# RMS normalisation on one core: last tile's load moved, squares, reductions and scaling dealt out anew

## The chip, the core and the metric

The kernel runs on one core of a Trainium2 chip. A core has TensorE (PE, matrix products), VectorE (DVE), ScalarE (ACT), GpSimd (POOL), SyncE (SP, which here only issues transfers) and 16 DMA engines, which move data between the main memory (HBM) and the on-chip memory SBUF. PSUM is a second, small on-chip memory; GpSimd is not used with it here. The engines run side by side and wait for each other by semaphores. The metric is the time of one execution on the device in microseconds (us), as the median of several runs.

## The reference

```python
batch, seq, dim = 16, 1024, 512      # x: float32; gamma: dim float32 values

def reference(x, gamma):
    eps = 1e-5
    rms = np.sqrt(np.mean(x ** 2, axis=-1, keepdims=True) + eps)
    return (x / rms * gamma).astype(np.float32)
```

Each of the 16384 rows of 512 values is divided by the root of its mean square and multiplied by gamma. 33.55 MB are read and 33.55 MB written.

## The kernel before

The 16384 rows are four tiles of 128 partitions x 32 rows x 512 values (64 KB per partition, 8 MB per tile). A partition's 32 rows lie one after the other in memory, so a transfer of n rows is 128 pieces of n x 2 KB. Three buffers `slot0` to `slot2` hold tiles 0, 1, 2; tile 3 uses `slot0` again, so its load must wait until tile 0 is stored.

All large transfers are issued by SP, in one queue: `load` (L42) and `store` (L45). SP works through its list in order, and a transfer whose data are not ready holds up what stands behind it. Their order is given by `transfers`: load 0 (8 rows, then 24), store row 0, load 1 (32), load 2 (16), store row 1 of tile 0, load 2 (16), store tile 0 (rows 2 to 32), store 1 (first 16), load 3 (16 and 16), store 1 (last 16), store 2 (32), store 3 (16 and 16).

A tile is worked on in four groups of 8 rows. For each group `row_stats` finds the sums of squares in one of two ways. In the first and third group of a tile ScalarE squares each row and accumulates its sum itself (L76, one instruction per row with an accumulator read behind it). In the second and fourth it squares four rows at a time into one of two PSUM buffers `sq` (L70), and VectorE adds them up (L71). ScalarE then takes the root (L82), and VectorE the reciprocal (L83). `apply` (L88) lets VectorE multiply each of the eight rows by its `rstd` and by `gamma_b`, in place, one instruction per row. gamma comes as one row by a small transfer; a matrix product with a column of ones spreads it over the partitions in PSUM, and VectorE copies it to `gamma_b` in SBUF (L57).

The main loop asks for the statistics of the next group ahead of scaling the current one. The order of instructions on each engine is that of a scheduler, which moves them within what the dependences allow: on VectorE, reductions and scaled rows of neighbouring groups are interleaved.

Of the kernel before, what the change touches and what calls it, by code (L numbers as in the profile page):

```python
# [1 line left out]

# [4 lines left out]


@with_exitstack
def kernel(  # L10
    ctx: ExitStack,
    tc: tile.TileContext,
    x: bass.AP,
    gamma: bass.AP,
    out: bass.AP,
):
    nc = tc.nc
    P = nc.NUM_PARTITIONS
    eps = 1e-5
    fp32 = mybir.dt.float32  # L20
    AF = mybir.ActivationFunctionType
    OP = mybir.AluOpType

    xf = x.flatten_outer_dims()
    of = out.flatten_outer_dims()
    N, D = xf.shape
    R = 32
    G = 8
    H = 4
    assert N == 4 * P * R  # L30

    xv = xf.rearrange("(t p r) d -> t p r d", p=P, r=R)
    ov = of.rearrange("(t p r) d -> t p r d", p=P, r=R)

    const = ctx.enter_context(tc.tile_pool(name="const", bufs=1))
    stats = ctx.enter_context(tc.tile_pool(name="stats", bufs=4))
    psum = ctx.enter_context(tc.tile_pool(name="psum", bufs=2, space=bass.MemoryType.PSUM))

    slots = [const.tile([P, R, D], fp32, name=f"slot{i}") for i in range(3)]

    def load(t, slot, r0, r1):
        nc.sync.dma_start(out=slots[slot][:, r0:r1], in_=xv[t][:, r0:r1])  # L42

    def store(t, slot, r0, r1):
        nc.sync.dma_start(out=ov[t][:, r0:r1], in_=slots[slot][:, r0:r1])  # L45

    load(0, 0, 0, 8)
    load(0, 0, 8, 32)

    gamma_row = const.tile([1, D], fp32)  # L50
    nc.scalar.dma_start(out=gamma_row, in_=gamma.unsqueeze(0))
    ones_col = const.tile([1, P], fp32)
    nc.vector.memset(ones_col, 1.0)  # L53
    gamma_psum = psum.tile([P, H, D], fp32, name="sq")
    nc.tensor.matmul(gamma_psum[:, 0], ones_col, gamma_row, start=True, stop=True)  # L55
    gamma_b = const.tile([P, D], fp32)
    nc.vector.tensor_copy(out=gamma_b, in_=gamma_psum[:, 0])  # L57

    eps_t = const.tile([P, 1], fp32)
    nc.vector.memset(eps_t, eps)  # L60
    sq_scratch = const.tile([P, D], fp32)

    def row_stats(slot, g):
        ss = stats.tile([P, G], fp32, name="ss")
        rms = stats.tile([P, G], fp32, name="rms")
        rstd = stats.tile([P, G], fp32, name="rstd")
        if (g // G) % 2:
            for h in range(0, G, H):
                sq = psum.tile([P, H, D], fp32, name="sq")
                nc.scalar.activation(out=sq, in_=slots[slot][:, g + h : g + h + H, :], func=AF.Square)  # L70
                nc.vector.tensor_reduce(  # L71
                    out=ss[:, h : h + H], in_=sq, axis=mybir.AxisListType.X, op=OP.add
                )
        else:
            for r in range(G):
                nc.scalar.activation(  # L76
                    out=sq_scratch,
                    in_=slots[slot][:, g + r, :],
                    func=AF.Square,
                    accum_out=ss[:, r : r + 1],  # L80
                )
        nc.scalar.activation(out=rms, in_=ss, func=AF.Sqrt, bias=eps_t, scale=1.0 / D)  # L82
        nc.vector.reciprocal(out=rstd, in_=rms)  # L83
        return rstd

    def apply(slot, g, rstd):
        for r in range(G):
            nc.vector.scalar_tensor_tensor(  # L88
                out=slots[slot][:, g + r, :],
                in0=slots[slot][:, g + r, :],  # L90
                scalar=rstd[:, r : r + 1],
                in1=gamma_b,
                op0=OP.mult,
                op1=OP.mult,
            )

    groups = [(t, g) for t in range(4) for g in range(0, R, G)]
    slot_of = [0, 1, 2, 0]

    def transfers(t, g):  # L100
        if (t, g) == (0, 0):
            store(0, 0, 0, 1)
            load(1, 1, 0, 32)
            load(2, 2, 0, 16)
            store(0, 0, 1, 2)
            load(2, 2, 16, 32)
        elif (t, g) == (0, 24):
            store(0, 0, 2, 32)
        elif (t, g) == (1, 8):
            store(1, 1, 0, 16)  # L110
            load(3, 0, 0, 16)
            load(3, 0, 16, 32)
        elif (t, g) == (1, 24):
            store(1, 1, 16, 32)
        elif (t, g) == (2, 24):
            store(2, 2, 0, 32)
        elif (t, g) == (3, 8):
            store(3, 0, 0, 16)
        elif (t, g) == (3, 24):
            store(3, 0, 16, 32)  # L120

    ahead = row_stats(0, 0)
    for k, (t, g) in enumerate(groups):
        rstd = ahead
        if k + 1 < len(groups):
            tn, gn = groups[k + 1]
            ahead = row_stats(slot_of[tn], gn)
        apply(slot_of[t], g, rstd)
        transfers(t, g)


# [1 line left out]
_INS = ['x', 'gamma']  # L133
_OUTS = [((16, 1024, 512), 'float32')]


# [23 lines left out]
```

## Time and profile before

| | us |
|---|---|
| median of 10 runs | 162.14 (161.91 to 162.45) |
| the profiled execution | 162.29 |
| its span (first to last record of the trace) | 160.5 |

| engine | busy in the span, us |
|---|---|
| VectorE: 128 scaled rows (L88) | 86.0 |
| VectorE: 16 reductions of 4 rows (L71) | 36.0 |
| ScalarE: 64 squares of one row (L76) and their 64 accumulator reads | 40.0 and 11.9 |
| ScalarE: 16 squares of 4 rows (L70) | 29.8 |
| ScalarE: 16 roots (L82) | 4.6 |

The busy time of a group is the sum of its instructions' own durations, which overlap a little: the next one starts before the last has quite ended. The DMA strip divides the span into 40 slices of 4 us and gives the mean busy share of the 16 DMA engines in tenths, 9 being 90% or more. The chain of waits follows the work that ended last back in time, at each step to what released it. It ends with the last compute instruction; a transfer issued after it is not in the chain.

Idle time that ScalarE spent waiting for VectorE's reductions (26.0 us before roots, 11.5 us before squares) and VectorE for ScalarE's roots (16.3 us) stands beside transfers that go on meanwhile.

### The profile page before, as it was taken

Reading aid. Unit: us, or ns where it says so; the run is one execution under the profiler, and the core shown is the slowest. Engines: PE = TensorE matmul, PEld = TensorE weight load, DVE = VectorE, ACT = ScalarE, POOL = GpSimd, SP = SyncE. Lnnn points to the kernel's source line nnn. Section 1 sums busy time; section 2 is a strip of 40 time slices with the busy share of each in tenths; the row PEclk is TensorE's granted clock in tenths of the full one; section 3 lists DMA queues with packets and bytes.
Section 4 is the critical chain, followed back from the end, with each engine's and each line's share of the span. In section 5 each row is a group of like instructions: output and inputs, shape, how many; then the busy total and the mean of one; then the engine's idle time right before and its main releaser. Section 6 shows DMA issues by size and latency. Waiting matters only on the chain.

```text
span 160.5 us, 409 instructions
## 1 busy us (share of the span) xinstructions
PE 2.0 (1%) x2; PEld 0.5 (0%) x2; DVE 122.6 (76%) x163; ACT 80.1 (50%) x162; POOL 0.2 (0%) x4
## 2 busy tenths in 40 slices
PE   3100000000000000000000000000000000000000
PEld 1000000000000000000000000000000000000000
DVE  0100937999999509999999999999999999995000
ACT  3099029991291999996900960079709940000000
POOL 0000000000000000000000000000000000000000
DMA  6999999699699999999899999999999899899993
GB/s 201 519 392 392 453 461 506 278 523 506 278 394 411 454 490 392 492 475 398 352 425 474 400 408 498 400 408 482 408 523 441 359 506 408 376 400 441 465 400 139
DMA packets 2164, 67.13 MB, mean 418 GB/s; under 512 B 241, under 2 KB 241, under 8 KB 498
## 3 DMA queue, kind: packets, MB, share of 16 engines
q1 hardware_dynamic: 2160, 67.11, 97.7%
q14 instruction: 2, 0.02, 0.0%
q10 hardware_dynamic: 2, 0.00, 0.0%
HBM read 33.56 MB, written 33.55 MB: 418 GB/s over the span
## 4 chain that ended last, share of the span: by engine, by line
DVE 64%; DMA 14%; ACT 11%; issue 2%; DVEq 0%; SPq 0%
DVE slot L88 45%; DVE ss L71 18%; DMA slot<-in_x_dram 14%; ACT sq_scratch L76 5%; ACT sq L70 5%; DVE rstd L83 1%; ACT rms L82 1%; DVEq L155 0%; SPq L42 0%
## 5 line engine op out<-in xcount | busy, mean ns | idle before, releaser
L88 DVE SCALAR_TENSOR_TENSOR slot<-slot,rstd,gamma_b 128x512 f32<-128x512 f32 x128 | 86.0, 748 | 0.1
L76 ACT ACTIVATE sq_scratch<-slot 128x512 f32<-128x512 f32 x64 | 40.0, 625 | 10.2 <-DMA slot<-in_x_dram 8.9
L70 ACT ACTIVATE sq<-slot 128x2048 f32<-128x2048 f32 x16 | 29.8, 1865 | 18.7 <-DVE ss L71 11.5
L71 DVE TENSOR_REDUCE ss<-sq 128x4 f32<-128x2048 f32 x16 | 36.0, 2284 | 3.5 <-ACT sq L70 3.5
L82 ACT ACTIVATE rms<-ss,eps_t 128x8 f32<-128x8 f32 x16 | 4.6, 297 | 26.2 <-DVE ss L71 26.0
L83 DVE RECIPROCAL rstd<-rms 128x8 f32<-128x8 f32 x16 | 3.2, 202 | 16.3 <-ACT rms L82 16.3
L76 ACT ACTIVATION_READ_ACCUMULATOR sq_scratch<-slot 128x1 f32 x64 | 11.9, 187 | 0.0
L57 DVE COPY gamma_b<-sq 128x512 f32<-128x512 f32 x1 | 0.7, 692 | 3.5 <-PE sq L55 3.5
L55 PE MATMUL sq<-gamma_row,ones_col 1*128 1x512 f32 x2 | 2.0, 1122 | 2.4 <-DMA gamma_row<-in_gamma_dram 2.4
L76 ACT ACT_TABLE_LOAD x1 | 1.3, 1283 | 1.3 <-PEq L144 1.3
L82 ACT ACT_TABLE_LOAD x1 | 1.3, 1283 | 0.0
L53 DVE MEMSET ones_col<- 1x128 f32 x1 | 0.2, 165 | 0.8 <-PEq L144 0.8
L55 PEld LDWEIGHTS sq<-gamma_row,ones_col 1*128 1x128 f32 x2 | 0.5, 306 | 2.4 <-issue 2.4
L144 POOL MEMSET const-bfloat16-1.0<- 128x1 bf16 x1 | 0.1, 101 | 0.0
L144 POOL MEMSET const-uint8-127<- 128x1 uint8 x1 | 0.1, 101 | 0.0
L144 POOL MEMSET const-float32-0.0<- 128x1 f32 x1 | 0.1, 98 | 0.2 <-issue 0.2
L144 POOL MEMSET const-float32-1.0<- 128x1 f32 x1 | 0.1, 98 | 0.0
L60 DVE MEMSET eps_t<- 128x1 f32 x1 | 0.1, 59 | 0.0
## 6 DMA issues: line engine op xcount, KB each, us to landing
slot<-in_x_dram SPq DMA_DIRECT2D x4, 4096.0 KB, 32.1
out_dram<-slot SPq DMA_DIRECT2D x4, 4096.0 KB, 18.5
out_dram<-slot SPq DMA_DIRECT2D x1, 7680.0 KB
slot<-in_x_dram SPq DMA_DIRECT2D x1, 6144.0 KB, 21.8
slot<-in_x_dram SPq DMA_DIRECT2D x1, 2048.0 KB, 7.4
out_dram<-slot SPq DMA_DIRECT2D x2, 256.0 KB, 21.2
gamma_row<-in_gamma_dram ACTq DMA_DIRECT2D x1, 2.0 KB
slot<-in_x_dram SPq DMA_DIRECT2D x1, 25.8
```

What stands on the lines that cost most here:

```text
L53: nc.vector.memset(ones_col, 1.0)
L55: nc.tensor.matmul(gamma_psum[:, 0], ones_col, gamma_row, start=True, stop=True)
L57: nc.vector.tensor_copy(out=gamma_b, in_=gamma_psum[:, 0])
L60: nc.vector.memset(eps_t, eps)
L70: nc.scalar.activation(out=sq, in_=slots[slot][:, g + h : g + h + H, :], func=AF.Square)
L71: nc.vector.tensor_reduce(out=ss[:, h : h + H], in_=sq, axis=mybir.AxisListType.X, op=OP.add)
L76: nc.scalar.activation(out=sq_scratch, in_=slots[slot][:, g + r, :], func=AF.Square, accum_out=ss[:, r : r + 1],)
L82: nc.scalar.activation(out=rms, in_=ss, func=AF.Sqrt, bias=eps_t, scale=1.0 / D)
L83: nc.vector.reciprocal(out=rstd, in_=rms)
L88: nc.vector.scalar_tensor_tensor(out=slots[slot][:, g + r, :], in0=slots[slot][:, g + r, :], scalar=rstd[:, r : r + 1], in1=gamma_b, op0=O ...
L144: nc = _bacc.Bacc("TRN2", target_bir_lowering=False, num_devices=1)
```

## The change

The order of instructions is now that of the source (`manual_schedule`), and VectorE's code begins at a multiple of 128 instruction slots (`addr_align`).

Work is dealt out anew. The groups are 8, 12 and 12 rows in tile 0 and 16 rows in the other tiles. ScalarE only squares, in pieces of 7, 5 and 4 rows, by turns into one PSUM buffer and one SBUF buffer, and takes the roots; the sums of all rows are VectorE's. Of each group the last rows (`share`: 3, 5, 5, 7, 7, 6, 6, 6, 3, in all 48 of 128) are scaled by GpSimd in two multiplications, by `rstd` and by gamma from SBUF. VectorE scales the others, one row per instruction as before, with gamma read from PSUM. ScalarE makes the SBUF copy of gamma, and GpSimd the two constants.

The transfers: the store of row 1 of tile 0 between the two halves of load 2 goes. Tile 0 is stored in rows 1 to 16 and 16 to 32, right after that tile 3 is loaded, then tile 1 is stored in one transfer of 128 pieces of 64 KB; tile 2 is stored in two halves.

```diff
+    ctx.enter_context(tc.manual_schedule())
+    nc.vector.addr_align(128, offset=0, max_nops=0)
...
-    nc.vector.tensor_copy(out=gamma_b, in_=gamma_psum[:, 0])
+    nc.scalar.copy(out=gamma_b[:, 0], in_=gamma_psum)
...
+    groups = [
+        (0, 0, 8, (4, 4), 3),
+        (0, 8, 12, (7, 5), 5),
+        (0, 20, 12, (7, 5), 5),
+        (1, 0, 16, (7, 5, 4), 7),
+        (1, 16, 16, (7, 5, 4), 7),
+        (2, 0, 16, (7, 5, 4), 6),
+        (2, 16, 16, (7, 5, 4), 6),
+        (3, 0, 16, (7, 5, 4), 6),
+        (3, 16, 16, (7, 5, 4), 3),
+    ]
...
+    def sum_squares(t, g, n, pieces, share):
+        ss = stats.tile([P, 16], fp32, name="ss")
+        r = 0
+        for k, m in enumerate(pieces):
+            if k % 2:
+                sq = const.tile([P, 5, D], fp32, name="sq_sbuf")
+            else:
+                sq = psum.tile([P, 7, D], fp32, name="sq_psum")
+            rows = slots[slot_of[t]][:, g + r : g + r + m, :]
+            nc.scalar.activation(out=sq[:, :m], in_=rows, func=AF.Square)
+            nc.vector.tensor_reduce(
+                out=ss[:, r : r + m], in_=sq[:, :m], axis=mybir.AxisListType.X, op=OP.add
+            )
+            r += m
+        return ss
...
+    def scale_by_pool(rstd, t, g, n, pieces, share):
+        part = slots[slot_of[t]][:, g + n - share : g + n, :]
+        by_row = rstd[:, n - share : n].to_broadcast([P, share, D])
+        nc.gpsimd.tensor_tensor(out=part, in0=part, in1=by_row, op=OP.mult)
+        nc.gpsimd.tensor_tensor(out=part, in0=part, in1=gamma_b.to_broadcast([P, share, D]), op=OP.mult)
...
+    def scale_row(rstd, t, g, r):
+        x = slots[slot_of[t]][:, g + r, :]
+        nc.vector.scalar_tensor_tensor(
+            out=x, in0=x, scalar=rstd[:, r], in1=gamma_psum, op0=OP.mult, op1=OP.mult
+        )
...
-            store(0, 0, 1, 2)
             load(2, 2, 16, 32)
-        elif (t, g) == (0, 24):
-            store(0, 0, 2, 32)
-        elif (t, g) == (1, 8):
-            store(1, 1, 0, 16)
+        elif (t, g) == (0, 20):
+            store(0, 0, 1, 16)
+            store(0, 0, 16, 32)
             load(3, 0, 0, 16)
             load(3, 0, 16, 32)
-        elif (t, g) == (1, 24):
-            store(1, 1, 16, 32)
-        elif (t, g) == (2, 24):
-            store(2, 2, 0, 32)
+        elif (t, g) == (1, 16):
+            store(1, 1, 0, 32)
+        elif (t, g) == (2, 0):
+            store(2, 2, 0, 16)
+        elif (t, g) == (2, 16):
+            store(2, 2, 16, 32)
...
+    for k, group in enumerate(groups):
+        t, g, n, pieces, share = group
+        rstd = ready
+        scale_by_pool(rstd, *group)
+        following = groups[k + 1 :][:1]
+        if k > 0:
+            for nxt in following:
+                ss = sum_squares(*nxt)
+        for r in range(n - share):
+            scale_row(rstd, t, g, r)
+            if r == 2 and k > 0:
+                for nxt in following:
+                    ready = inverse_rms(ss, nxt[2])
         transfers(t, g)
+        if k == 0:
+            for nxt in following:
+                ready = inverse_rms(sum_squares(*nxt), nxt[2])
```

So on VectorE each group's scaled rows stand behind the reductions of the next group, except the first three rows' place before the next reciprocal: reductions of the next group, three rows, reciprocal of the next group, the other rows.

## The prediction

> **What bounds the kernel now.** I read the DMA part of the page first, because the kernel moves 67 MB and computes little per byte.
>
> ```profile
> PE 2.0 (1%) x2; PEld 0.5 (0%) x2; DVE 122.6 (76%) x163; ACT 80.1 (50%) x162; POOL 0.2 (0%) x4
> DMA  6999999699699999999899999999999899899993
> q1 hardware_dynamic: 2160, 67.11, 97.7%
> DVE 64%; DMA 14%; ACT 11%; issue 2%; DVEq 0%; SPq 0%
> ```
>
> The 16 DMA engines are busy for 97.7% of the span on one queue, idle only in the first slice and at the end of the last. No compute engine is above 76%. The chain of waits nevertheless puts 64% on DVE. The reader should see that both can hold: the chain ends with VectorE's last rows releasing the last store, but that store then stands in a queue that is still full. The stretches of the trace (length, then each engine's busy time, granted clock, DMA share, GB/s) and the issues in the stretches from 105 and from 147 us show how full:
>
> ```profile
> 22.00:61.00 39.00, 0.00 (x0) 0.00 (x0) 30.64 (x35) 27.55 (x48) 0.00 (x0) 1.00 1.00 432
> 61.00:158.00 97.00, 0.00 (x0) 0.00 (x0) 85.53 (x117) 43.88 (x96) 0.00 (x0) 1.00 1.00 431
> ...
> 60.00:62.00 2.00, 0.00 (x0) 0.00 (x0) 2.00 (x2) 1.94 (x7) 0.00 (x0) 1.00 0.87 328
> ```
> ```profile
> 116.13 31.03 SPq L45 DMA_DIRECT2D out_dram<-slot  x3
> 131.69 15.46 SPq L45 DMA_DIRECT2D out_dram<-slot  x2
> out_dram<-slot SPq DMA_DIRECT2D x1, 24.2
> out_dram<-slot SPq DMA_DIRECT2D x2, 4096.0 KB, 15.6
> out_dram<-slot SPq DMA_DIRECT2D x1, 4096.0 KB, 12.9
> ```
>
> From 22 to 158 us the share is 1.00 at 431 to 432 GB/s. Tile 2's store (8 MB) is issued at 116.1 and lands 24.2 us later, at 140.3. The two halves of tile 3 are issued at 131.7 and 146.8. The second lands after 12.9 us, at 159.7; as the middle of the two is 15.6, the first takes 18.3 and lands at 150.0. A 4 MB half alone needs 4.19 MB / 432 GB/s = 9.7 us, exactly the distance of these landings. So the queue never runs dry, and the program ends 0.8 us after the last landing, at 160.5. The fixed ends are a start of about 2 us and this tail; the rest is bytes.
>
> How late may a store be issued without a hole? The first load (2.1 MB, 4.9 us of data) lands 7.4 us after its issue, so an empty queue costs at most 2.5 us of lead. A half of tile 3 thus has to be issued 9.7 + 2.5 = 12.2 us before the landing it has now: by 137.8 for the first half (150.0) and 147.5 for the second (159.7). Before, the second is issued at 146.8, 0.7 us to spare.
>
> [...] The COPY from PSUM in this trace takes 692 ns[...].
>
> **The change, part by part.**
>
> *Transfers.* Before there are 15 transfers of tiles, after also 15, with the same bytes in one queue. One 2 KB-row store goes; tile 0's store is cut in two, tile 1's two halves become one, tile 2's store becomes two halves. With the number of packets (128 each) unchanged, bigger rows in one place are paid back by smaller ones in another: 0. The store of row 1 no longer stands between the halves of tile 2's load, so one turn from loading to storing goes. The turn at 61 us costs 2 us x (1 - 328/432) = 0.5 us; the one that goes is tiny, I take 0.2 us (0 to 0.5). Order of SP: load 3 now stands behind tile 0's two stores alone; its waits are their landings, about 72 and 82 us, while the queue holds work to about 81 and 91. Behind these waits on SP stands tile 1's store, which is not ready before 90. No hole. Each store now waits for VectorE and for GpSimd.
>
> *ScalarE.* 64 squares with accumulator reads (40.0 + 11.9 us) and 16 squares of four rows (29.8) become 26 squares. The slope from the two rows is (1865 - 625) / 1536 = 0.81 ns per element, so 7 rows are 3.1 us, 5 rows 2.3, 4 rows 1.87: 57 us in all. ScalarE goes off the path except where tile 0's second group waits for its single PSUM buffer.
>
> *VectorE.* All 128 rows are now reduced there, in place of 64; 80 rows are scaled, in place of 128. The durations come from these rows:
>
> ```profile
> 120.99 10.68 DVE L88 SCALAR_TENSOR_TENSOR slot<-slot,rstd,gamma_b 128x512 f32<-128x512 f32 x16
> 116.10 4.41 DVE ss L71 x2
> L57 DVE COPY gamma_b<-sq 128x512 f32<-128x512 f32 x1 | 0.7, 692 | 3.5 <-PE sq L55 3.5
> L71 DVE TENSOR_REDUCE ss<-sq 128x4 f32<-128x2048 f32 x16 | 36.0, 2284 | 3.5 <-ACT sq L70 3.5
> ```
>
> A scaled row costs 10.68 / 16 = 0.66 us start to start (its 748 ns overlap the next). A reduction of 4 rows costs 2.20[...]. A reciprocal costs 0.11. A group of 16 rows with 7 given to GpSimd is 8.74 + 9 x 0.66 + 0.11 = 14.8 us, with 6 given 15.45.
>
> Now the line of time. The first square of the 24-row load starts at 23.0 as before (landing). Squares of 7 rows to 26.2, reductions of 7 and 5 (3.80 + 2.74) to 32.7, root and reciprocal to 33.1. The next square of 7 rows is behind that root on ScalarE: VectorE stalls until 36.1. Reductions to 42.7; three rows, a reciprocal, four rows to 47.4. Then reductions of 16 rows to 56.2 and seven rows to 60.9: tile 0 is done. Tile 1: 75.7 and 90.5. Tile 2: 105.9 and 121.4. Tile 3's first half: 136.8. Its last 13 rows: 145.4. Against the deadlines: tile 0's first store can go at 47.4 and its second at 60.9 (needed about 60 and 70), tile 1's at 90.5 (needed by about 98), tile 2's halves at 105.9 and 121.4 (needed by about 118 and 128), tile 3's at 136.8 and 145.4 (needed by 137.8 and 147.5). The tightest spare is 1.0 us. At the start, squares of 4 + 4 rows from 8.2, two reductions, table load and root put the first scaled row at about 17.0, so load 1 is issued near 18; the queue holds the 24-row load until 22.
>
> *GpSimd.* 48 rows in two passes. [...] From tile 1's reciprocal at 58.2 it works without a break[...]. It stays inside VectorE's cover. From both sides: a tenth faster changes nothing; it delays the third-last store above (137.8 - 58.2) / 32768 = 2.43 ns per element.
>
> *Scale from PSUM.* The row's gamma now comes from PSUM. Unknown: 0 by the COPY row[...]. I take 0[...].
>
> *Instructions not in the diff.* GpSimd's program gets a reload of its library before the first multiply, in the idle time to 16 us. [...] I take 0.
>
> *Code address, fixed order.* From 61 us to its last row at 146.8 VectorE is busy 85.5 of 85.8 us, so next to nothing is lost to instruction supply: 0. Fewer instructions could save a fetch on the DMA engines, which is inside the 0.2.
>
> Sum: 162.29 (the profiled execution, span 160.5) - 0.2 = 162.1. That execution lies 0.15 above the median of the runs (162.14), so 161.9 for a median.
>
> **Rivals.**
> 1. *VectorE pays for PSUM* (slower). 62 scaled rows lie between tile 0's second group and the first half of tile 3. [...] It decides above 1.0 us / 62 = 16 ns per row. [...] Against: the COPY row.
> 2. *GpSimd becomes the bound.* [...] For: nothing in this trace shows GpSimd's rate. [...]
> 3. *The library's bytes* go first through a queue that is full[...].
> 4. *The turns and fetches give more*: a whole 0.5 us turn and the last engine's lag, 161.2.
>
> **How the numbers follow.** Forecast 0.60, rivals 0.18, 0.09, 0.08 and 0.05. A measurement of this kernel tells about 0.2% (0.32 us) from no change. The forecast, -0.2 with an uncertainty of about 0.35 us, splits into 0.22 faster, 0.34 same, 0.04 slower. Rival 4 adds 0.05 to faster; of rival 1 and 3 small prices add 0.02 to same. Together 0.27, 0.36, 0.37. The range runs from 161.2 to 165.0: it takes in rivals 1 and 3 up to their full price and leaves out rival 2 and the tails. The likeliest case's own range is 161.4 to 162.4.
>
> **What would show it.** DMA share 1.00 from 22 to 158 us, and the first half of tile 3 issued before 138 us, confirm the forecast. Scaled rows over 0.68 us apart and a hole in the DMA share near 140 us mean rival 1. GpSimd rows over 17 us per seven rows, with stores waiting on POOL, mean rival 2. More bytes on the instruction queue in the first 20 us mean rival 3. The prediction is wrong if a store is issued into an empty queue anywhere.

## The result, and the profile after

The changed kernel takes 163.86 us (median of 8 runs, 163.6 to 164.06), the kernel before 162.12 beside it: a ratio of 1.0106, with a 95% interval of 1.0096 to 1.0117. The forecast was no measurable change, 161.9. The profiled execution took 163.89 with a span of 162.2, 1.7 us more than before. These lines of the page after answer to those shown of before (engine busy times, the DMA strip, its queues, the chain, the costliest groups):

```profile
PE 2.0 (1%) x2; PEld 0.5 (0%) x2; DVE 123.8 (76%) x113; ACT 63.5 (39%) x36; POOL 96.6 (60%) x24
DMA  5998989699698998999989989959969999999880
q1 hardware_dynamic: 2160, 67.11, 96.7%
q14 instruction: 1, 0.01, 0.0%
DVE 68%; DMA 14%; ACT 4%; issue 3%; DVEq 0%; SPq 0%
L108 DVE SCALAR_TENSOR_TENSOR slot<-slot,rstd,gamma_psum 128x512 f32<-128x512 f32 x80 | 53.5, 750 | 0.0
L97 DVE RECIPROCAL rstd<-rms 128x16 f32<-128x16 f32 (+2 forms) x9 | 2.2, 247 | 2.1 <-ACT rms L96 2.1
```

Nearly every line looks as forecast. VectorE has the same load, the queue moves the same 2160 packets, and a row scaled from PSUM takes 750 ns against 748. Six such rows beside GpSimd at work, twenty at the end, and GpSimd's two passes over six rows of a group:

```profile
72.89 3.96 DVE L108 SCALAR_TENSOR_TENSOR slot<-slot,rstd,gamma_psum 128x512 f32<-128x512 f32 x6
133.07 13.19 DVE L108 SCALAR_TENSOR_TENSOR slot<-slot,rstd,gamma_psum 128x512 f32<-128x512 f32 x20
L104 POOL TENSOR_TENSOR slot<-slot,gamma_b 128x3072 f32<-128x3072 f32 x3 | 20.0, 6662 | 0.2
L103 POOL TENSOR_TENSOR slot<-slot,rstd 128x3072 f32<-128x3072 f32 x3 | 15.9, 5309 | 6.2 <-DVE rstd L97 6.2
```

The stretches (length, busy time of each engine, clock, DMA share, GB/s) and the two last stores show no hole in the DMA work either:

```profile
22.00:61.00 39.00, 0.00 (x0) 0.00 (x0) 30.42 (x23) 22.04 (x12) 22.88 (x6) 1.00 1.02 436
61.00:100.00 39.00, 0.00 (x0) 0.00 (x0) 39.00 (x31) 18.97 (x10) 38.43 (x6) 1.00 0.99 428
100.00:140.00 40.00, 0.00 (x0) 0.00 (x0) 40.00 (x44) 15.30 (x9) 30.13 (x6) 1.00 1.00 432
140.00:158.00 18.00, 0.00 (x0) 0.00 (x0) 6.26 (x10) 0.00 (x0) 0.00 (x0) 1.00 0.99 428
```
```profile
137.77 0.33 SPq L46 DMA_DIRECT2D out_dram<-slot  x1
out_dram<-slot SPq DMA_DIRECT2D x1, 4096.0 KB, 13.8
146.33 0.33 SPq L46 DMA_DIRECT2D out_dram<-slot  x1
out_dram<-slot SPq DMA_DIRECT2D x1, 4096.0 KB, 14.9
```

The halves of tile 3 land at 151.6 and 161.2, each 1.5 us later than before (150.0 and 159.7), though the first was issued inside the deadline of 137.8. What differs is the very end of the queue. The windows of half a microsecond behind 158 us, first of before, then of after:

```profile
158.00:158.50 0.50, 0.00 (x0) 0.00 (x0) 0.00 (x0) 0.00 (x0) 0.00 (x0) 1.00 0.17 66
158.50:159.00 0.50, 0.00 (x0) 0.00 (x0) 0.00 (x0) 0.00 (x0) 0.00 (x0) 1.00 0.00 0
159.50:160.00 0.50, 0.00 (x0) 0.00 (x0) 0.00 (x0) 0.00 (x0) 0.00 (x0) 1.00 0.00 0
```
```profile
158.00:158.50 0.50, 0.00 (x0) 0.00 (x0) 0.00 (x0) 0.00 (x0) 0.00 (x0) 1.00 0.01 0
158.50:159.00 0.50, 0.00 (x0) 0.00 (x0) 0.00 (x0) 0.00 (x0) 0.00 (x0) 1.00 0.15 66
159.50:160.00 0.50, 0.00 (x0) 0.00 (x0) 0.00 (x0) 0.00 (x0) 0.00 (x0) 1.00 0.15 66
```

A packet is counted where it starts, and 66 GB/s over 0.5 us is 33 KB: a single packet of the last store. Before, the last one starts by 158.5. After, one packet still starts at 158.5 to 159 and one more at 159.5 to 160. The page gives the mean of 16 engines. The trace's packet records can be put into 16 chains, read here as one for each engine: a packet begins where the one before it has ended, and every transfer of 128 packets of data gives each chain eight. In the changed kernel 15 chains finish by 158.5 and the last at 160.9. In the kernel before 14 finish by 158.5, one at 158.8 and the last at 159.4. The last store lands 0.3 us behind its last chain in both (161.2 and 159.7): it is done when the last engine is. The middle of the 16 ends its part of the last store at 158.2 before and at 158.3 after. So the queue as a whole is as fast as before, and the loss is the lag of one engine behind the middle one: 1.14 us before, 2.68 after.

On that last engine's chain of after lies the 8 KB packet of queue 14, at 3.8 us. Before, two such packets lie at 47 and 65 us, on the two chains that end at 158.8 and 159.4:

```profile
q14 instruction: 1, 0.01, 1.0%
```

This line is the answer for 3 to 5 us of after; for 46 to 48 and for 64 to 66 us of before it reads the same. The trace names the queue "instruction", and the packet stands in the middle of an engine's chain: it takes 0.31 us from 3.80, and a packet of the first load follows at 4.11, which takes 1.14 us, 0.53 more than others (0.61). Then the last packets of the loads take longer on this engine than on the rest: near 21 us 0.95 us over the usual time where the others have about 0.4, near 61 us 1.23 where they have about 0.3.

From turn to turn the last engine of the changed kernel falls further behind the middle one: 0.9 us at the end of the first load, 1.5 near 22 us, 2.5 near 62, 2.7 near 100. The early lag also reaches the compute engines. The first square of the 24-row load starts at 23.02 in the kernel before (first line) and at 24.19 after:

```profile
23.02 3.68 ACT L70 ACTIVATE sq<-slot 128x2048 f32<-128x2048 f32 x2 [7.24 <-DMA slot<-in_x_dram]
24.19 3.16 ACT L86 ACTIVATE sq_psum<-slot 128x3584 f32<-128x3584 f32 x1 [7.31 <-DMA slot<-in_x_dram]
```

**Theory A**: the aligned start makes VectorE's next block of instructions come over the DMA engines among the first loads. That puts one engine behind, and each later turn from loading to storing widens its lag. **Rivals**: B, GpSimd's library reload is the early packet; C, GpSimd's work beside the transfers slows them; D, only the number of fetches counts, not their time.

### The profile page after: what moved, and what is told of

It reads as the page before. It is cut to its first block, busy times and chain, and to the rows that moved or that the text cites. A ratio compares the mean times of both kernels' runs of the same rounds, so it can differ in the third digit from the quotient of the medians.

```text
span 162.2 us, 273 instructions
## 1 busy us (share of the span) xinstructions
PE 2.0 (1%) x2; PEld 0.5 (0%) x2; DVE 123.8 (76%) x113; ACT 63.5 (39%) x36; POOL 96.6 (60%) x24
## 3 DMA queue, kind: packets, MB, share of 16 engines
q1 hardware_dynamic: 2160, 67.11, 96.7%
## 4 chain that ended last, share of the span: by engine, by line
DVE 68%; DMA 14%; ACT 4%; issue 3%; DVEq 0%; SPq 0%
DVE ss L87 38%; DVE slot L108 29%; DMA slot<-in_x_dram 14%; ACT sq_psum L86 4%; DVE rstd L97 1%; DVEq L177 0%; SPq L43 0%; ACT rms L96 0%
## 5 line engine op out<-in xcount | busy, mean ns | idle before, releaser
L103 POOL TENSOR_TENSOR slot<-slot,rstd 128x3072 f32<-128x3072 f32 (+3 forms) x9 | 42.6, 4738 | 41.7 <-DVE rstd L97 41.7
L87 DVE TENSOR_REDUCE ss<-sq_psum 128x7 f32<-128x3584 f32 (+1 forms) x15 | 47.2, 3149 | 20.4 <-ACT sq_psum L86 20.4
L104 POOL TENSOR_TENSOR slot<-slot,gamma_b 128x3072 f32<-128x3072 f32 (+3 forms) x9 | 53.5, 5949 | 0.7
L108 DVE SCALAR_TENSOR_TENSOR slot<-slot,rstd,gamma_psum 128x512 f32<-128x512 f32 x80 | 53.5, 750 | 0.0
L86 ACT ACTIVATE sq_psum<-slot 128x3584 f32<-128x3584 f32 (+1 forms) x15 | 38.3, 2555 | 35.2 <-DVE ss L87 23.8
L87 DVE TENSOR_REDUCE ss<-sq_sbuf 128x5 f32<-128x2560 f32 (+1 forms) x9 | 24.8, 2759 | 0.0
L86 ACT ACTIVATE sq_sbuf<-slot 128x2560 f32<-128x2560 f32 (+1 forms) x9 | 20.5, 2274 | 0.0
L96 ACT ACTIVATE rms<-ss,eps_t 128x16 f32<-128x16 f32 (+2 forms) x9 | 2.8, 306 | 27.1 <-DVE ss L87 27.0
L97 DVE RECIPROCAL rstd<-rms 128x16 f32<-128x16 f32 (+2 forms) x9 | 2.2, 247 | 2.1 <-ACT rms L96 2.1
L56 PE MATMUL gamma_psum<-gamma_row,ones_col 1*128 1x512 f32 x2 | 2.0, 1120 | 2.1 <-DMA gamma_row<-in_gamma_dram 2.1
```

What stands on the lines that cost most here:

```text
L56: nc.tensor.matmul(gamma_psum, ones_col, gamma_row, start=True, stop=True)
L86: nc.scalar.activation(out=sq[:, :m], in_=rows, func=AF.Square)
L87: nc.vector.tensor_reduce(out=ss[:, r : r + m], in_=sq[:, :m], axis=mybir.AxisListType.X, op=OP.add)
L96: nc.scalar.activation(out=rms[:, :n], in_=ss[:, :n], func=AF.Sqrt, bias=eps_t, scale=1.0 / D)
L97: nc.vector.reciprocal(out=rstd[:, :n, 0], in_=rms[:, :n])
L103: nc.gpsimd.tensor_tensor(out=part, in0=part, in1=by_row, op=OP.mult)
```

## The experiments

All times are medians; each ratio is to the kernel before on the same chip.

**Without the aligned start.**

```diff
-    nc.vector.addr_align(128, offset=0, max_nops=0)
```

> The changed kernel without the aligned start of VectorE's code; nothing else differs. Theory A (the aligned start makes one 8 KB block of instructions come through the DMA engines at about 4 us, puts one of the 16 engines behind the others, and each turn from loading to storing widens that lag): the instruction packet leaves the first 10 us, the last store packets start before 158.5 us again, the first 24-row load lands near 23.0 instead of 24.2, and the time is 162.0 to 162.6. Theory B (the early packet belongs to GpSimd's library or to GpSimd's work): packet and tail stay, 163.7 to 164.0. Theory C (the lag comes from work of GpSimd beside the transfers, whatever the packet): the packet goes, the time stays above 163.4.

Measured: 162.81, ratio 1.0047 (1.0031 to 1.0062), 1.05 us below the changed kernel. The first square of the 24-row load and the only instruction packet (88 to 90 us):

```profile
22.77 3.16 ACT L85 ACTIVATE sq_psum<-slot 128x3584 f32<-128x3584 f32 x1 [6.61 <-DMA slot<-in_x_dram]
```
```profile
q14 instruction: 1, 0.01, 1.0%
```

The early packet belongs to the alignment, which costs most of the loss (1.05 of 1.74 us), and the load lands 1.4 us earlier. B and C fall for this part. The time is above the expected span: 0.7 us remain, with a fetch now among tile 3's loads.

**The alignment in the kernel before.**

```diff
+    nc.vector.addr_align(128, offset=0, max_nops=0)
```

> The kernel before with the aligned start of VectorE's code added; nothing else differs. Theory A: an 8 KB instruction packet in the first 10 us, one lagging engine, first 24-row load landing about 1 us later, 163 to 164. Theory B: no such packet, 162.1 within 0.3.

Measured: 164.41, ratio 1.0147 (1.0117 to 1.0178): 2.3 us for the one line in a kernel without any multiplication on GpSimd, more than was expected. The trace has instruction packets at 3.6, 48.4 and 100.8 us. The one at 48.4 answers to that at 47 in the kernel before; VectorE's at 65 us is gone, and the other two stand in its place.

**The first turn taken out of the changed kernel.**

```diff
-            store(0, 0, 0, 1)
...
-            store(0, 0, 1, 16)
+            store(0, 0, 0, 16)
```

> The changed kernel without the early store of row 0 of tile 0 (that row goes with rows 1 to 16), so that the turn from loading to storing near 21 us is gone and load 1 no longer waits for group 0. Theory A: the early instruction packet stays and its engine is 0.5 us behind, but the widening at 21 us (one load packet there took 0.95 us longer) is gone: the 24-row load lands near 23, and the time falls by about 0.5 to 1 us to 162.9 to 163.4. If the turns do not matter and the lag is set by the packet alone, 163.7 to 163.9.

Measured: 163.97, ratio 1.0117 (1.0093 to 1.014), no gain: a miss. The slow packet at 21 us is gone, and until 51 us the engine stays 0.9 us behind. But near 59 us a load packet of the same engine takes 1.67 us over the usual time (1.23 near 61 us in the changed kernel), and the other engines' last load packets there take up to 0.9 us more. Behind the turn near 61 us the lag is 1.5 us, behind that near 100 us 2.5, and the middle engine ends 0.4 us later than in the changed kernel. The first turn is thus no fixed charge.

**The library reload in the kernel before.**

```diff
+    lib = const.tile([P, 1], fp32)
+    nc.gpsimd.memset(lib, 1.0)
+    nc.gpsimd.tensor_tensor(out=lib, in0=lib, in1=lib, op=OP.mult)
```

> The kernel before with one multiplication of 128 x 1 values on GpSimd near the start, whose program thereby gets the library reload that the changed kernel has. Theory A: no early instruction packet, no change, 162.1 within 0.3. Theory B (the reload fetches over the DMA engines): an 8 KB packet near 4 us or more bytes, and 163 or more.

Measured: 162.09, ratio 1.0001 (0.9989 to 1.0012), packets at 47 and 65 us as before. GpSimd's record has the two MODIFY_POOL_CONFIG instructions ahead of its multiplication that the changed kernel has and the kernel before lacks. What they bring is free here; B falls.

**The fetch moved by padding.** VectorE gets n memsets in front, in time in which it waits for the first load anyway (its first reduction in the changed kernel stands at 10.72 us):

```diff
+    pad_t = const.tile([P, 1], fp32)
+    for _ in range(n):
+        nc.vector.memset(pad_t, 0.0)
```

with n = 26, 37, 61 and 13, on top of the kernel without alignment:

> The kernel of e1_no_align with 26 tiny memsets (128 x 1) ahead on VectorE, which is idle there, so that its code crosses into the next block of 128 instructions earlier. Theory A (what counts is when the 8 KB block is fetched: among loads it costs its DMA engine about 0.6 us, among stores 0.3, and the lag grows at every later turn from loading to storing): the packet comes at 64 to 67 us, among stores, just behind the turn near 61, with one turn left: 162.1 to 162.6, that is 0.2 to 0.7 below e1_no_align. Theory D (only the number of fetches counts, one in either): 162.8 as in e1_no_align.

> The same with 37 memsets, so that the packet comes at about 51 to 55 us, among loads and ahead of the turns near 61 and 100 us. Theory A: lag of about 0.6 and two turns, slower than e1_no_align, 163.2 to 163.8. Theory D: 162.8.

> The same with 61 memsets, so that the packet comes at about 5 to 12 us without any aligned address, ahead of all three turns. Theory A: the changed kernel's time without its alignment, 163.6 to 164.1, and the first 24-row load lands near 24. Theory D: 162.8. If the alignment itself had slowed VectorE or its supply of instructions, also 162.8.

> The kernel of e1_no_align with 13 tiny memsets ahead on VectorE, so that the packet comes near 64 us, among tile 0's stores, with one turn left. Theory A: as e1_no_align or a little below, 162.4 to 162.9, and clearly below the 163.5 of the kernels whose packet comes at 42 and 47 us with two turns left. If memsets at the start or any other address cost the time by themselves, 163.5.

With 26 the packet came at 47 us and not at 64 to 67, so that this run fell among the loads like the next one and its expected time does not apply; my count of the instructions up to the fetch was wrong. It took 163.63 (1.0069 to 1.0102). With 37 it came at 42 us: 163.50 (1.0072 to 1.0101). With 61 at 11 us: 164.07 (1.0104 to 1.0134), without any alignment. With 13 at 75 us, among stores: 162.44 (1.0006 to 1.0028). D falls: each of these has one packet ahead of the end of the work, and their times differ by 1.6 us.

**The fetch behind the last turn.** On top of the kernel without alignment, this one leaves out the scaling of 47 of VectorE's 80 rows:

```diff
         for r in range(n - share):
-            scale_row(rstd, t, g, r)
+            if k > 5:
+                scale_row(rstd, t, g, r)
```

> The kernel of e1_no_align without the rows that VectorE scales in the first six groups (47 of 80 rows are left unscaled; transfers, squares, sums and GpSimd's rows as before). VectorE's code is 47 instructions shorter, so the 8 KB block is fetched only after tile 3 has landed, past the last turn from loading to storing, or not at all. Theory A: no engine lags at a turn, the last packets start within about 0.5 us of the others' and the time is 161.6 to 162.2, at or below the kernel before. Theory D (GpSimd beside the transfers, or the order of the transfers, costs the remaining 0.7 us of e1_no_align): 162.8.

Measured: 162.06, ratio 0.9997 (0.9989 to 1.0005): the whole loss against the kernel before is gone. The packet lies at 124 us (answer for 123 to 125 us), and no packet starts behind 158.5:

```profile
q14 instruction: 1, 0.01, 1.0%
```
```profile
158.00:158.50 0.50, 0.00 (x0) 0.00 (x0) 0.00 (x0) 0.00 (x0) 0.00 (x0) 1.00 0.01 0
158.50:159.00 0.50, 0.00 (x0) 0.00 (x0) 0.00 (x0) 0.00 (x0) 0.00 (x0) 1.00 0.00 0
159.50:160.00 0.50, 0.00 (x0) 0.00 (x0) 0.00 (x0) 0.00 (x0) 0.00 (x0) 1.00 0.00 0
```

**The control for the work left out**, the same with the aligned start:

```diff
+    nc.vector.addr_align(128, offset=0, max_nops=0)
```

> The kernel of e9 (47 of VectorE's rows left unscaled) with VectorE's code aligned again: the control for the work left out. Theory A: packet near 4 us ahead of all turns, 163.5 to 164.1 as the changed kernel. If e9 was fast because VectorE had less to do, 162.1.

Measured: 164.08, ratio 1.0122 (1.0103 to 1.0141). The two single packets at the end are back:

```profile
158.50:159.00 0.50, 0.00 (x0) 0.00 (x0) 0.00 (x0) 0.00 (x0) 0.00 (x0) 1.00 0.15 66
159.50:160.00 0.50, 0.00 (x0) 0.00 (x0) 0.00 (x0) 0.00 (x0) 0.00 (x0) 1.00 0.15 66
```

With 47 rows fewer on VectorE the alignment still costs 2.0 us (164.08 - 162.06). It is neither VectorE's lateness nor its lighter load that decides. GpSimd's rows, the squares and the transfers are the same in both, so C falls too.

**ScalarE's code aligned**, with VectorE's (first) and in its place (second):

```diff
+    nc.scalar.addr_align(128, offset=0, max_nops=0)
```

> The changed kernel with ScalarE's code aligned in the same way, so that two blocks are fetched early. Theory A with the last engine deciding: if the two fetches go over different DMA engines, the slower one decides and the time stays 163.7 to 164.2; if over the same one, the lags add up and it is 164.5 or more. If the mean load of the 16 engines decided, 0.02 us more.

> The kernel of e1_no_align with ScalarE's code aligned in place of VectorE's. Theory A (any 8 KB block fetched among the first loads puts its DMA engine behind, whichever engine's code it is): packets near 4 and near 89 us; if both are served by one DMA engine or the early one costs as much as VectorE's, 163.6 to 164.2. If the early block of ScalarE comes before the loads have filled the queue, or costs nothing, 162.8 as e1_no_align.

Measured: ratios 1.0081 (1.0053 to 1.0109) and 1.0071 (1.0044 to 1.0099). The intervals lie between, or touch, the values that the expectations set apart, the runs behind them spread widely (162.48 to 164.19 and 162.66 to 163.98), and ScalarE's packet comes at 1.8 us, just when the first load starts. No sum of two lags is seen in the first. Its trace is that of its fastest run, 162.48, and shows a turn that widens nothing: the engine with VectorE's packet, at 3.6 us, is 0.9 us behind near 22 us and 0.8 at the end. The packet at 47 us in the kernel before is alike, 0.5 us behind at once and 0.6 at the end. So a fetch ahead of a turn does not always cost more.

The runs with a single fetch of VectorE ahead of the end, in the order of its time, with the lag of the last engine behind the middle one at the end of the traced execution:

| packet at, us | turns still to come | median, us | ratio, 95% interval | lag, us |
|---|---|---|---|---|
| 3.8 (changed kernel) | 3 | 163.86 | 1.0096 to 1.0117 | 2.68 |
| 3.6 (rows left out) | 3 | 164.08 | 1.0103 to 1.0141 | 2.74 |
| 11.2 | 3 | 164.07 | 1.0104 to 1.0134 | 2.76 |
| 42.1 | 2 | 163.50 | 1.0072 to 1.0101 | 2.11 |
| 47.1 | 2 | 163.63 | 1.0069 to 1.0102 | 2.55 |
| 74.8 (among stores) | 1 | 162.44 | 1.0006 to 1.0028 | 1.02 |
| 89.1 (among loads) | 1 | 162.81 | 1.0031 to 1.0062 | 1.35 |
| 124.4 (rows left out) | 0 | 162.06 | 0.9989 to 1.0005 | 0.60 |

In all eight traces the last engine is the one whose chain holds the packet, and the traced execution's time less its lag is 161.2 to 161.5 us, in the kernel before 161.15. So the lag of one engine accounts for the differences. With the same number of turns to come the medians lie within 0.4 us, though the two with one turn have intervals apart. From two turns to one they fall by 0.7 to 1.2 us, from one to none by 0.4 to 0.8; from three to two only by 0.2 to 0.6, with intervals that partly overlap.

## Why the prediction was wrong

- *Transfers at equal cost, no hole*: right. The moved load, the 64 KB rows and the turn that goes cost nothing together: the middle engine ends at 158.2 before and 158.3 after. The 0.2 us that I took for the turn did not come. That 432 GB/s is the most that the steady stretch gives was not shown; its stretches after have 428 to 436.
- *VectorE from PSUM*: right. Twenty rows take 13.19 us, 0.66 each, as before, and one row by itself 750 ns against 748; rival 1 had no part. The zero was my estimate from the one COPY from PSUM (692 ns); the trace of before has no copy from SBUF to set beside it.
- *VectorE's reductions*: right. The 8.74 us for the 16 rows of a group was an estimate (four times the 2.20 us of a 4-row reduction before is 8.80). From start to start, pieces of 7, 5 and 4 rows take 3.80, 2.73 and 2.19 us in the changed kernel (from 48.63 us on), 8.72 in all.
- *GpSimd*: it stayed inside VectorE's cover as forecast: its last pass ends at 139.5 us, VectorE's last row at 146.3. How fast it would be, nothing in the trace of before showed. The pass by gamma took 6662 ns for 3072 elements, 2.17 ns each; the pass by `rstd`, where one value serves a row, 5309 ns, 1.73 each. Both are below the 2.43 from which I expected a late store. VectorE's rows kept their spacing beside it (3.96 us for six at 72.9 us, 0.66 each).
- *Line of time*: tile 3's first half was issued at 137.8, forecast 136.8. The load landed 1.2 us later than I assumed, which is the lag of the one engine; I had taken the landing of before.
- *Library reload*: right, nothing (1.0001). What the trace shows of it are the two MODIFY_POOL_CONFIG instructions, at 0.91 and 0.94 us in the changed kernel; that they stand for a reload was my reading, and no run shows what it moves or how long it takes. The sign set for rival 3, more bytes on the instruction queue in the first 20 us, did appear, as one packet; it was VectorE's.
- *Code address*: this is the step that failed. I priced the alignment at 0 because VectorE loses no time to its supply of instructions, and put a saved fetch inside 0.2 us. Both are true of VectorE, which is busy 79.00 of the 79 us from 61 to 140, and of the mean, whose share there is 0.99 and 1.00. But the block comes over a DMA engine of a kernel that its DMA engines bound, and the alignment moved it from 89 us, among tile 3's loads, to 3.8 us, among the first loads and ahead of all turns. That is 1.05 us of the 1.74 us lost. The other 0.7 us goes when the fetch moves from 89 to 124 us. The kernel before pays for such fetches too, at 47 and 65 us (lag 1.14 us), so that 162.12 is not a time without them.
- Behind it stands a reading error: a mean share of 1.00 over 16 engines was taken as the bound. The bound is the last engine (before, it ends at 159.4 us and the middle one at 158.2). Rival 4 named the last engine's lag, but only as something that the change could take away.
- *Range*: 163.86 lies inside 161.2 to 165.0, in the part that was kept for rivals 1 and 3, whose prices no run had shown. Neither had a share, so this is luck.

What stays open: how, and when, a turn widens a lag. The packet records show the late engine's last load packets taking longer (by 1.23 us near 61 us in the changed kernel) while the others already store. But taking out the first turn did not help, and two traces show lags that did not grow, so the widening is not a fixed price per turn. Whether another engine's early fetch costs the same was not settled. A version with all its work and the fetch behind the last turn, which would need some 15 instructions of VectorE fewer before 103 us (14 lie between the fetch at 89 us and there), was not built; the run at 124 us gives no reason to expect less than the time of before.

## What to carry to other kernels

When the DMA engines bound a kernel, ask for the last of them and not for their mean (here the last ended 2.68 us behind the middle one): look at the packets of the final microseconds, and at queue 14. The place of an instruction block counted here (164.08 us with the fetch at 3.6 us, 162.06 with it at 124): look for a place in which VectorE's code is not fetched among loads that still have turns ahead, and measure an alignment against the same kernel without it. An edit that costs an engine nothing can still cost the queue that feeds it: the aligned start took 1.05 us here, with VectorE busy without a break from 61 to 140 us.

## What had not been expected of the hardware

- One 8 KB instruction packet (0.31 us on one of 16 engines) costs 2.0 us more of a 162 us kernel at 3.6 us than at 124 us (164.08 against 162.06), several times its own length.
- Such a packet came about once per 128 recorded instructions of VectorE: in the changed kernel behind the 3rd and, at 162.9 us, behind the last, the 132nd; with 61 memsets behind the 64th and the 192nd; in the kernel before with the alignment 106 lie between.
- The same single line costs 1.05 us in the changed kernel and 2.3 us in the kernel before, where VectorE's code then needs a second fetch, at 100.8 us.
